# Mixing and turning heads in the middle of a weight block, and the last pooling passes cut off from GpSimd's adds and held in program order

## The chip, the core and the metric

The kernel runs on one core of one Trainium2 chip. The metric is device time in microseconds (us), the median of several runs. Five engines work side by side, each through its own list of instructions: TensorE (PE, matrix products), VectorE (DVE), ScalarE (ACT), GpSimd (POOL) and SyncE (SP, which issues the DMAs here).

## The reference, cut to what matters

One layer with 512 positions and 1024 channels. A normalised input `hn` is projected into three mixers (A, B, C) and three gates, the mixers' outputs are merged and projected, and a SwiGLU layer and a gated embedding follow. The change touches A and C.

```
# A: spatial gating, 8 heads of 128 channels, 4 blocks of 128 positions
u, v = split(gelu(z_sgu))
v = layer_norm(v, g_v, b_v)
mixed = einsum('hij,bnjhc->bnihc', w, v) + b_s      # one 128x128 matrix per head
br_a = (u * mixed) @ w_sgu_out
# B: depthwise convolution, width 31: 31 multiply-adds ("taps") per channel tile
# C: pooling with windows 2, 4, 8, 16 on four groups of 256 channels
outs.append((c - prev) / cnt - zf)                  # trailing mean minus the input
br_c = (einsum('bsgc,gcd->bsgd', pooled, w_pool) * s_pool) @ w_pool_out
...
merged = gates[0] * br_a + gates[1] * br_b + gates[2] * br_c
```

## The kernel before, in words

Channels lie on the 128 partitions, so a tile of a product is 128 channels by 512 positions. Every float32 operand of a product is split into a rounded part `hi` (a cast on ACT) and the rest `lo` (a subtraction on DVE), and each product is three matmuls (hi·hi, hi·lo, lo·hi: `mm3`). Weights stream in blocks of 128x1024: a DMA into `raw`, then `split` into `hi` and `lo`. A weight block is 24 matmuls.

The instructions are written by a scheduler: it takes the program in the order in which it is written, estimates times, and may reorder instructions on an engine, except where `order()` (or `drain`) keeps them in program order. On the chip, each engine then runs its list as it stands. Nearly all lines show as L69, that of the helper that issues them, so the names of tiles tell the steps apart.

- `natural` (L433) computes the two halves of A, `v_all` first and `u_all` second, with positions on the partitions. For each half of the columns (`c` = 0, 1) it holds four PSUM banks `ps_nat`, one per block of positions, and takes four weight blocks (`kk` = 0 to 3). After each weight block it drains some convolution taps from `background`, and yields.
- `v_all` is normalised on DVE (`v_norm`, `v_gain`), and GpSimd adds the bias (`v_all<-v_all,b_bc`), while the products of `u_all` run.
- `mix_head(h)` splits one head of `v_all` (`v_split`, hi on ACT, lo on DVE), multiplies it with the head's matrix (`ps_mix`, three matmuls) and lets DVE form `gated` from it. `turn_head(h)` transposes `gated` on PE (`ps_tr`, four small matmuls) and splits it (`sgu`). Heads 0 to 3 are mixed, and 0 and 1 turned, inside `natural` for `u_all` at `c` = 1, the rest between the gate tiles that follow (`ps_gate`).
- For C, `z_all` is computed in eight tiles (`ps_z`). After each pair, `pool_windows` (L570) lets GpSimd add shifted copies (`win`, 1 to 4 adds and as many small copies, for windows 2 to 16). Then three passes on DVE divide, and subtract `z_all`: two short ones for the first positions (`win<-win,rcnt` and `win<-win,z_all` of a few elements) and a long one (128x2x510 down to 128x2x496). `win` is then split into `pl_hi` and `pl_lo`, and `pool_map` multiplies that with the group's weights (`ps_pool`, twelve matmuls, of which the first two need `pl_hi` alone, and ten stand together behind them).
- The taps of the convolution (`acc<-h_conv,vec,acc`, DVE, one tile of 512 positions each) fill up DVE: 4 are drained after each block in `u_all`, 3 after a `z` tile, 5 after a gate tile. `drain` puts them in program order. When a tile is done, GpSimd adds it to `conv_sum`.

Of the kernel before, what the change touches and what calls it, by code (L numbers as in the profile page):

```python
# [13 lines left out]
ALU = mybir.AluOpType  # L14
# [7 lines left out]
NB = T // P  # L22
# [4 lines left out]
WINDOWS = (2, 4, 8, 16)  # L27
GROUPS = (0, 1, 2, 3)
# [53 lines left out]
def hybrid_block(  # L82
# [8 lines left out]
    order = InOrder(tc)  # L91
    dve, act_e, pe = order.engine(nc.vector), order.engine(nc.scalar), order.engine(nc.tensor)
# [9 lines left out]
    def bank(name):  # L102
        return psum.tile([P, T], F32, tag="ps", name=name)

    def wide_tile(name):
        return wide.tile([P, KT, T], F32, tag="wide", name=name)

    def slot(tag, name, dt=F32R, shape=(2, T)):
        return act.tile([P, *shape], dt, tag=tag, name=name, bufs=6 if tag == "tm" else 8)

    def t2(name, n=T):
        return tmp.tile([P, n], F32, tag="t2", name=name)
# [23 lines left out]
    def col(name, k):  # L136
        i = VECS.index(name) * KT + k
        return vec[:, i:i + 1]
# [23 lines left out]
    def split(hi, lo, src):  # L162
        act_e.copy(hi, src)
        dve.tensor_tensor(out=lo, in0=src, in1=hi, op=ALU.subtract)

    def split_scaled(hi, lo, src, scale):

        act_e.activation(out=hi, in_=src, func=AF.Copy, scale=scale)
        dve.scalar_tensor_tensor(out=lo, in0=src, scalar=scale, in1=hi,
                                       op0=ALU.mult, op1=ALU.subtract)  # L170
# [36 lines left out]
    def mm3(out, wh, wl, xh, xl, first, last):  # L207
        pe.matmul(out, lhsT=wh, rhs=xh, start=first, stop=False)
        pe.matmul(out, lhsT=wh, rhs=xl, start=False, stop=False)
        pe.matmul(out, lhsT=wl, rhs=xh, start=False, stop=last)  # L210
# [4 lines left out]
    def product(ps, w, acts, hs=FULL, k0=0, last=True):  # L215

        hi, lo = w
        for i, a in enumerate(acts):
            mm3(ps[:, hs], blk(hi, i), blk(lo, i), a[:, 0, hs], a[:, 1, hs],
                k0 + i == 0, last and i == len(acts) - 1)  # L220
# [11 lines left out]
    def drain(n):  # L232
        for _ in range(min(n, len(background))):
            with order():
                background.pop(0)()
# [72 lines left out]
    POOL_LAG = 3  # L308
# [107 lines left out]
    for i in range(KT):  # L416
        t = t2("nrm")
        dve.scalar_tensor_tensor(out=t, in0=x_all[:, i], scalar=col("g_mix_pre", i),
                                       in1=x_inv, op0=ALU.mult, op1=ALU.mult)
# [13 lines left out]
    def natural(dst, evacuate, taps):  # L433

        for c in range(2):
            banks = [bank("ps_nat") for _ in range(NB)]
            for kk in range(4):
                hi, lo = weights.get()
                for b in range(NB):
                    ts = slice(b * P, (b + 1) * P)  # L440
                    for j in range(2):
                        k = 2 * kk + j
                        a = hn[k]
                        ws = slice(j * T, (j + 1) * T)
                        pe.matmul(banks[b], lhsT=a[:, 0, ts], rhs=hi[:, ws],
                                         start=k == 0, stop=False)
                        pe.matmul(banks[b], lhsT=a[:, 1, ts], rhs=hi[:, ws],
                                         start=False, stop=False)
                        pe.matmul(banks[b], lhsT=a[:, 0, ts], rhs=lo[:, ws],
                                         start=False, stop=k == KT - 1)  # L450
                drain(taps)
                if kk == 3:
                    for b in range(NB):
                        evacuate(dst, b, c, banks[b])
                yield c, kk

    def blocks_of(t):
        return t.rearrange("p a b -> p (a b)").rearrange("p (n c) -> p n c", n=NB)
# [13 lines left out]
    for _ in natural(v_all, v_gelu, TAPS[1]):  # L472
        pass
# [31 lines left out]
    def mix_head(h):  # L505
        cs = slice(h * P, (h + 1) * P)
        vs = slot("tm", "v_split", shape=(2, NB, P))
        split(vs[:, 0], vs[:, 1], v_all[:, :, cs])
        ps = bank("ps_mix")
        mm3(ps, sg_hi[:, cs], sg_lo[:, cs], vs[:, 0], vs[:, 1], True, True)  # L510
        gated[h] = t2("gated")
        with order():
            dve.scalar_tensor_tensor(
                out=gated[h].rearrange("p (n c) -> p n c", n=NB),
                in0=ps.rearrange("p (n c) -> p n c", n=NB),
                scalar=col("b_sgu_s", h), in1=u_all[:, :, cs], op0=ALU.add, op1=ALU.mult)

    def turn_head(h):
        pt = bank("ps_tr")
        for b in range(NB):  # L520
            bs = slice(b * P, (b + 1) * P)
            pe.transpose(out=pt[:, bs], in_=gated[h][:, bs], identity=ident)
        sgu_T[h] = slot("br", f"sgu{h}")
        split(sgu_T[h][:, 0], sgu_T[h][:, 1], pt)

    for c, kk in natural(u_all, u_gelu, TAPS_U):
        if c == 1:
            if kk > 1:
                turn_head(kk - 2)
            mix_head(kk)  # L530


    merged = wide_tile("merged")
# [1 line left out]
    def gate_tile(dst, taps, between=None):  # L535
        ps = bank("ps_gate")
        w = weights.get()
        half = KT // 2 if between else KT
        product(ps, w, hn[:half], last=not between)
        if between:  # L540
            between()
            product(ps, [h[:, half * P:] for h in w], hn[half:], k0=half)
        act_e.activation(out=dst, in_=ps, func=AF.Sigmoid)
        drain(taps)
# [21 lines left out]
    z_all = wide_tile("z_all")  # L566
    pool_T = [None] * KT
    pooled = [None] * 4

    def pool_windows(gi):  # L570
        w = WINDOWS[gi]
        z = z_all[:, 2 * gi:2 * gi + 2, :]
        cur, d = z, 1
        while d < w:
            nxt = slot("tm", "win", F32)
            nc.gpsimd.tensor_tensor(out=nxt[:, :, d:], in0=cur[:, :, d:], in1=cur[:, :, :T - d], op=ALU.add)
            nc.gpsimd.tensor_copy(nxt[:, :, :d], cur[:, :, :d])
            cur, d = nxt, 2 * d
        head = rcnt[:, None, :w].broadcast_to([P, 2, w])
        dve.tensor_tensor(out=cur[:, :, :w], in0=cur[:, :, :w], in1=head, op=ALU.mult)  # L580
        dve.tensor_tensor(out=cur[:, :, :w], in0=cur[:, :, :w], in1=z[:, :, :w], op=ALU.subtract)
        dve.scalar_tensor_tensor(out=cur[:, :, w:], in0=cur[:, :, w:], scalar=1.0 / w,
                                       in1=z[:, :, w:], op0=ALU.mult, op1=ALU.subtract)
        hi = slot("tm", "pl_hi")
        lo = slot("tm", "pl_lo")
        split(hi, lo, cur)
        pooled[gi] = hi, lo

    def pool_map(gi):
        wh, wl = weights.get()  # L590
        hi, lo = pooled[gi]
        for j in range(2):
            n = 2 * gi + j
            ps = bank("ps_pool")
            for k in range(2):
                s = slice(k * 256 + j * P, k * 256 + (j + 1) * P)
                mm3(ps, wh[:, s], wl[:, s], hi[:, k], lo[:, k], k == 0, k == 1)
            pool_T[n] = slot("br", f"pool{n}")
            split_scaled(pool_T[n][:, 0], pool_T[n][:, 1], ps, col("s_pool", n))

    for g in GROUPS:
        for n in (2 * g, 2 * g + 1):
            ps = bank("ps_z")
            product(ps, weights.get(), hn)
            act_e.copy(z_all[:, n, :], ps)
            drain(TAPS[3])
        pool_windows(g)
        if 0 < g < GROUPS[-1]:
            pool_map(g - 1)

    gates = []
    for n in range(KT + POOL_LAG):
        if n < KT:
            gates.append(t2("gate"))
            gate_tile(gates[n], TAPS[4], (lambda: pool_map(GROUPS[-2])) if n == 0 else None)
        if n == POOL_LAG - 1:
            pool_map(GROUPS[-1])
        if n >= POOL_LAG:
            i = n - POOL_LAG
            ps = branch_tile(pool_T, TAPS[4])  # L620
            t = t2("br")
            dve.tensor_tensor(out=t, in0=ps, in1=gates[i], op=ALU.mult)
            nc.gpsimd.tensor_tensor(out=merged[:, i, :], in0=merged[:, i, :], in1=t, op=ALU.add)
# [94 lines left out]
    with order():  # L718
# [6 lines left out]
        for i in range(N_HALF):  # L725
            n = KT - N_HALF + i
            add_mixed(mix_tile(n, late[i], lo_half), n, lo_half)
        sqs = []
        for i in range(N_HALF):
            n = KT - N_HALF + i  # L730
# [71 lines left out]
    def evacuate(ps, n, hs):  # L802
        act_e.activation(out=o2_all[:, n, hs], in_=ps[:, hs], func=AF.Copy, scale=col("g_ffn_post", n))
        add_square(f_sums[:, hs], ps[:, hs], n, dve)
# [32 lines left out]
    with order():  # L837
# [3 lines left out]
        w = weights.get(1)  # L841
        for b, hs in zip(halves, HALVES):
            ffn_out(b, KT - 1, 0, w, hs)
        w = weights.get(1)
        ffn_out(ps, KT - 2, 1, w)
        weights.ahead(3)
        w = weights.get(2)
# [41 lines left out]
        for n in range(N_LAST, KT):  # L889
            w = weights.get()  # L890
# [70 lines left out]
```

## Time and profile before

| | |
|---|---|
| median of 3 runs | 984.22 us (984.08 to 984.52) |
| the profiled execution | 983.63 us, of which the span from the first instruction to the last is 981.9 us |
| granted TensorE clock | 1.000 over the span |
| PE busy | 973.8 us (99%), 4682 matmuls |
| DVE busy | 677.3 us (69%), 903 instructions |
| ACT busy | 346.1 us (35%) |
| POOL busy | 88.2 us (9%), 64 instructions |
| DMA | 100.53 MB, mean 102 GB/s |

In a line of the timeline the columns are the start, the duration, the engine, the line in the code, the operation with the tile written and the tiles read, shapes, the number of merged instructions, and in brackets the idle time of the engine ahead of it and what ended that. The list of waits gives total us, number of waits and the longest.

### The profile page before, as it was taken

The numbers are of one execution on the slowest core, as the hardware profiler recorded it, in microseconds if no ns is written. First come the engines' busy times: TensorE is split into PE (matmuls) and PEld (weight loads), VectorE is DVE, ScalarE is ACT, GpSimd is POOL, SyncE is SP. The second block draws the span as 40 slices with busy tenths as digits, with TensorE's granted clock in tenths as the row PEclk, the third lists the DMA queues.
The fourth block names the chain that finished last, engine by engine and source line by source line (L and its number), as shares of the span: only waits on it lengthen the run. The fifth ranks groups of instructions, "written<-read, shape, count | busy, mean of one in ns | idle before, by whom it ended". The sixth has DMA issues, their size and how long they took to land.

```text
span 981.9 us, 11718 instructions
## 1 busy us (share of the span) xinstructions
PE 973.8 (99%) x4682; PEld 819.2 (83%) x4682; DVE 677.3 (69%) x903; ACT 346.1 (35%) x483; POOL 88.2 (9%) x64
## 2 busy tenths in 40 slices
PE   9999999999999999999999999999999999999998
PEld 6788888788888878888888998888888888888897
DVE  7898789999988899957555787544444432223575
ACT  6422333332224332146435443323232322223442
POOL 4000004000013712160000010000000000000000
PEclk9999999999999999999999999999999999999999
DMA  6433331323322322332338112323322333334312
GB/s 233 137 108 107 109 106 65 107 69 104 107 81 81 101 103 86 105 110 68 126 96 272 62 38 74 104 90 104 98 96 93 98 91 104 92 92 139 109 43 86
DMA packets 30006, 100.53 MB, mean 102 GB/s; under 512 B 3456, under 2 KB 3968, under 8 KB 29952
## 3 DMA queue, kind: packets, MB, share of 16 engines
q1 hardware_dynamic: 29808, 99.75, 30.9%
q8 instruction: 36, 0.59, 0.2%
q14 instruction: 18, 0.15, 0.0%
q10 hardware_dynamic: 144, 0.04, 0.0%
HBM read 97.68 MB, written 2.10 MB: 102 GB/s over the span
## 4 chain that ended last, share of the span: by engine, by line
PE 88%; DVE 7%; issue 2%; DMA 1%; ACT 1%; SPq 0%; DVEq 0%; ACTq 0%
PE ps_f L69 25%; PE ps_br L69 13%; PE ps_fo L69 12%; PE ps_gate L69 12%; PE ps_ag L69 5%; PE ps_pg L69 5%; PE ps_o L69 5%; PE ps_z L69 4%; PE ps_nat L69 4%; DVE lo L69 2%; DVE acc L69 2%; PE ps_ple L69 1%; PE ps_pool L69 1%; DVE v_all L69 1%; DMA first_all<-in_w_first 1%
## 5 line engine op out<-in xcount | busy, mean ns | idle before, releaser
L69 ACT CAST hi<-raw 128x1024 fp32r<-128x1024 f32 (+3 forms) x158 | 162.5, 1030 | 456.3 <-PE ps_br L69 88.4
L69 DVE TENSOR_TENSOR lo<-raw,hi 128x1024 fp32r<-128x1024 f32 (+3 forms) x158 | 206.2, 1306 | 107.0 <-ACT hi L69 106.5
L69 DVE SCALAR_TENSOR_TENSOR acc<-h_conv,vec,acc 128x511 f32<-128x511 f32 (+14 forms) x240 | 183.3, 764 | 5.2
L69 PE MATMUL ps_f<-hg,hi 128*128 128x512 f32 (+1 forms) x624 | 184.5, 379 | 0.0
L69 PEld LDWEIGHTS ps_f<-hg,hi 128*128 128x128 f32 x624 | 115.1, 188 | 21.7
L69 PE MATMUL ps_gate<-hn,hi 128*128 128x512 f32 x384 | 119.6, 392 | 0.9 <-DVE gated L69 0.9
L69 PE MATMUL ps_f<-hg,lo 128*128 128x512 f32 (+1 forms) x312 | 118.0, 379 | 0.0
L69 PE MATMUL ps_fo<-f,hi 128*128 128x512 f32 (+1 forms) x396 | 111.0, 366 | 0.0
L69 PEld LDWEIGHTS ps_gate<-hn,hi 128*128 128x128 f32 x384 | 72.0, 188 | 17.1 <-DVE gated L69 1.3
L69 PEld LDWEIGHTS ps_fo<-f,hi 128*128 128x128 f32 x396 | 71.7, 189 | 12.2
L69 PE MATMUL ps_nat<-hi,hn 128*128 128x512 f32 x256 | 78.8, 390 | 0.0
L69 PE MATMUL ps_gate<-hn,lo 128*128 128x512 f32 x192 | 74.9, 390 | 0.0
L69 PE MATMUL ps_fo<-f,lo 128*128 128x512 f32 (+1 forms) x198 | 72.5, 366 | 0.0
L69 PEld LDWEIGHTS ps_f<-hg,lo 128*128 128x128 f32 x312 | 58.7, 188 | 11.0
L69 PEld LDWEIGHTS ps_nat<-hi,hn 128*128 128x128 f32 x256 | 48.1, 188 | 10.0
L69 DVE TENSOR_TENSOR f<-ps_f,h_inv 128x512 f32<-128x512 f32 x22 | 15.2, 690 | 56.5 <-PE ps_f L69 56.5
L69 PE MATMUL ps_nat<-lo,hn 128*128 128x512 f32 x128 | 49.9, 390 | 0.0
L69 PE MATMUL ps_ag<-hn,hi 128*128 128x512 f32 x160 | 49.6, 391 | 0.2 <-DVE sig L69 0.2
L69 PEld LDWEIGHTS ps_fo<-f,lo 128*128 128x128 f32 x198 | 37.4, 189 | 6.0
L69 PEld LDWEIGHTS ps_gate<-hn,lo 128*128 128x128 f32 x192 | 36.1, 188 | 7.5
L69 DVE TENSOR_TENSOR silu<-ps_f,h_inv 128x512 f32<-128x512 f32 x22 | 15.2, 690 | 36.0 <-PE ps_f L69 35.9
L69 PE MATMUL ps_br<-pool,hi 128*128 128x512 f32 x128 | 39.6, 389 | 0.0
(214 smaller groups left out, 1566.5 us busy)
## 6 DMA issues: line engine op xcount, KB each, us to landing
raw<-in_w_mix SPq DMA_DIRECT2D x90, 512.0 KB, 3.2
raw<-in_w_ffn_in SPq DMA_DIRECT2D x44, 512.0 KB, 3.3
raw<-in_w_ffn_out SPq DMA_DIRECT2D x16, 448.0 KB, 3.3
raw<-in_w_ffn_out SPq DMA_DIRECT2D x8, 512.0 KB, 3.5
raw<-in_w_ple_gate SPq DMA_DIRECT2D x8, 512.0 KB, 4.2
x_all<-in_xT SPq DMA_DIRECT2D x8, 256.0 KB, 6.4
h_all<-in_xT SPq DMA_DIRECT2D x4, 512.0 KB, 5.2
out_dram<-pg SPq DMA_DIRECT2D x7, 256.0 KB, 2.0
```

The costliest lines, as they stand in the source:

```text
L69: inst = op(*args, **kw)
```

## The change

`natural` yields in the middle of a weight block, ahead of the third of its four blocks of positions, where it yielded at the end of it. What the loop over `u_all` does at a yield comes twelve matmuls (half a block) earlier in the program. In that loop `mix_head` stands ahead of `turn_head`.

`pool_windows` keeps only GpSimd's adds. The three DVE passes and the split move to a new function, `pool_mean`, and are held in program order. They are called later: for group 0 after the z tile 2, for group 1 after tile 4, for group 2 after tile 7, and for group 3 after the gate tile 1, each time behind the taps that this tile drained.

```
             for kk in range(4):
                 hi, lo = weights.get()
                 for b in range(NB):
+                    if b == NB // 2:
+                        yield c, kk
                     ts = slice(b * P, (b + 1) * P)
...
-                yield c, kk
...
         if c == 1:
+            mix_head(kk)
             if kk > 1:
                 turn_head(kk - 2)
-            mix_head(kk)
...
             cur, d = nxt, 2 * d
+        pooled[gi] = cur
+
+    def pool_mean(gi):
+        w = WINDOWS[gi]
+        z, cur = z_all[:, 2 * gi:2 * gi + 2, :], pooled[gi]
         head = rcnt[:, None, :w].broadcast_to([P, 2, w])
-        dve.tensor_tensor(out=cur[:, :, :w], in0=cur[:, :, :w], in1=head, op=ALU.mult)
-        dve.tensor_tensor(out=cur[:, :, :w], in0=cur[:, :, :w], in1=z[:, :, :w], op=ALU.subtract)
-        dve.scalar_tensor_tensor(out=cur[:, :, w:], in0=cur[:, :, w:], scalar=1.0 / w,
-                                       in1=z[:, :, w:], op0=ALU.mult, op1=ALU.subtract)
+        with order():
+            dve.tensor_tensor(out=cur[:, :, :w], in0=cur[:, :, :w], in1=head, op=ALU.mult)
+            dve.tensor_tensor(out=cur[:, :, :w], in0=cur[:, :, :w], in1=z[:, :, :w], op=ALU.subtract)
+            dve.scalar_tensor_tensor(out=cur[:, :, w:], in0=cur[:, :, w:], scalar=1.0 / w,
+                                           in1=z[:, :, w:], op0=ALU.mult, op1=ALU.subtract)
         hi = slot("tm", "pl_hi")
         lo = slot("tm", "pl_lo")
         split(hi, lo, cur)
...
             drain(TAPS[3])
+            if g and n == 2 * g + (g == GROUPS[-1]):
+                pool_mean(g - 1)
         pool_windows(g)
...
             gate_tile(gates[n], TAPS[4], (lambda: pool_map(GROUPS[-2])) if n == 0 else None)
+        if n == POOL_LAG - 2:
+            pool_mean(GROUPS[-1])
         if n == POOL_LAG - 1:
             pool_map(GROUPS[-1])
```

No instruction is added or taken away, and the lists of SP (DMAs) and GpSimd keep their order. On PE, DVE and ACT rows move. In the rows below a name is the tile written, then the tiles read; a minus is a row of before, a plus one of the change.

PE, in the first weight block of `c` = 1 of `u_all`, the first mix (head 0):

```order
 L69 MATMUL ps_nat<-hi,hn_228 128x512 x2
 L69 MATMUL ps_nat<-lo,hn_228 128x512
-L69 MATMUL ps_nat<-hi,hn_227 128x512 x2
+L69 MATMUL ps_mix<-v_split,w_hi 128x512
+L69 MATMUL ps_nat<-hi,hn_227 128x512
+L69 MATMUL ps_mix<-v_split,w_hi 128x512
+L69 MATMUL ps_mix<-v_split,w_lo 128x512
+L69 MATMUL ps_nat<-hi,hn_227 128x512
 L69 MATMUL ps_nat<-lo,hn_227 128x512
 L69 MATMUL ps_nat<-hi,hn_228 128x512 x2
```

The three `ps_mix` matmuls stood behind all 24 matmuls of the block; now the first stands behind 12 of them, and the other two behind 13. On ACT and DVE the splits of the first two heads keep their places.

DVE, the passes of group 2 (window 8), before:

```order
L69 SCALAR_TENSOR_TENSOR pool_2449<-ps_pool,vec,pool_2449 128x512
L69 SCALAR_TENSOR_TENSOR acc_225<-h_conv_221,vec,acc_225 128x485
L69 TENSOR_TENSOR lo<-raw,hi 128x512
L69 SCALAR_TENSOR_TENSOR win<-win,z_all 128x2x504
L69 TENSOR_TENSOR win<-win,rcnt 128x2x8
L69 SCALAR_TENSOR_TENSOR acc_225<-h_conv_221,vec,acc_225 128x484
L69 TENSOR_TENSOR win<-win,z_all 128x2x8
L69 SCALAR_TENSOR_TENSOR acc_225<-h_conv_221,vec,acc_225 128x483
L69 SCALAR_TENSOR_TENSOR acc_225<-h_conv_221,vec,acc_225 128x482
L69 TENSOR_TENSOR pl_lo<-win,pl_hi 128x1024
```

and in the change (`pool_2432` and `pool_2442` are the two results of group 1's `pool_map`):

```order
L69 SCALAR_TENSOR_TENSOR pool_2432<-ps_pool,vec,pool_2432 128x512
L69 TENSOR_TENSOR lo<-raw,hi 128x1024
L69 SCALAR_TENSOR_TENSOR acc_225<-h_conv_221,vec,acc_225 128x486
L69 TENSOR_TENSOR lo<-raw,hi 128x512
L69 SCALAR_TENSOR_TENSOR pool_2442<-ps_pool,vec,pool_2442 128x512
L69 SCALAR_TENSOR_TENSOR acc_225<-h_conv_221,vec,acc_225 128x485
L69 SCALAR_TENSOR_TENSOR acc_225<-h_conv_221,vec,acc_225 128x484
L69 SCALAR_TENSOR_TENSOR acc_225<-h_conv_221,vec,acc_225 128x483
L69 SCALAR_TENSOR_TENSOR acc_225<-h_conv_221,vec,acc_225 128x482
L69 TENSOR_TENSOR win<-win,rcnt 128x2x8
L69 TENSOR_TENSOR lo<-raw,hi 128x1024
L69 TENSOR_TENSOR win<-win,z_all 128x2x8
```

The long pass (128x2x504) is the next row. It moved behind the tile's last three taps (`acc` 484 to 482), and the last of these lets GpSimd add to `conv_sum`.

DVE, the passes of group 3 (window 16), before:

```order
L69 SCALAR_TENSOR_TENSOR pool_2584<-ps_pool,vec,pool_2584 128x512
L69 TENSOR_SCALAR acc_226<-h_conv_222,vec 128x512
L69 SCALAR_TENSOR_TENSOR acc_226<-h_conv_222,vec,acc_226 128x511
L69 SCALAR_TENSOR_TENSOR acc_226<-h_conv_222,vec,acc_226 128x510
L69 SCALAR_TENSOR_TENSOR win<-win,z_all 128x2x496
L69 TENSOR_TENSOR win<-win,rcnt 128x2x16
L69 SCALAR_TENSOR_TENSOR acc_226<-h_conv_222,vec,acc_226 128x509
L69 TENSOR_TENSOR win<-win,z_all 128x2x16
```

and in the change, where ahead of these rows stand `pool_2567`, a `lo` of 128x512, `pool_2577` (group 2's results), the first tap 128x512, a `lo` of 128x1024 and the taps 511 to 509:

```order
L69 SCALAR_TENSOR_TENSOR acc_226<-h_conv_222,vec,acc_226 128x508
L69 SCALAR_TENSOR_TENSOR acc_226<-h_conv_222,vec,acc_226 128x507
L69 TENSOR_TENSOR lo<-raw,hi 128x1024
L69 SCALAR_TENSOR_TENSOR acc_226<-h_conv_222,vec,acc_226 128x506
L69 SCALAR_TENSOR_TENSOR acc_226<-h_conv_222,vec,acc_226 128x505
L69 SCALAR_TENSOR_TENSOR acc_226<-h_conv_222,vec,acc_226 128x504
L69 SCALAR_TENSOR_TENSOR acc_226<-h_conv_222,vec,acc_226 128x503
L69 TENSOR_TENSOR win<-win,rcnt 128x2x16
L69 SCALAR_TENSOR_TENSOR acc_226<-h_conv_222,vec,acc_226 128x502
L69 TENSOR_TENSOR win<-win,z_all 128x2x16
L69 SCALAR_TENSOR_TENSOR win<-win,z_all 128x2x496
```

The long pass stood behind three taps of this tile and stands behind eleven. On PE the first `ps_pool` of group 3 keeps its place, right behind the third gate tile. The ten matmuls of group 2's `ps_pool` moved up toward it: with them, 58 matmuls stood from their first to group 3's first, and 37 stand there now. From the ten of group 1 to the first of group 2 there are 59, and from the ten of group 0 to the first of group 1 there are 46 (the ten counted in).

## The prediction

> **What bounds the kernel now.** I read the page first, then the waits of TensorE (PE), then the timeline at the places of the change, engine by engine.
>
> ```profile
> span 981.9 us, 11718 instructions
> PE 973.8 (99%) x4682; PEld 819.2 (83%) x4682; DVE 677.3 (69%) x903; ACT 346.1 (35%) x483; POOL 88.2 (9%) x64
> PE 88%; DVE 7%; issue 2%; DMA 1%; ACT 1%; SPq 0%; DVEq 0%; ACTq 0%
> ```
>
> PE is busy for 99% of the span and makes 88% of the chain that ended last. So time can only come from PE's waits or go into new ones. Its own list of waits, and a row of the chain that gives the pace:
>
> ```profile
> PE ps_gate L69 <- DVE gated L69: 0.9, 1, 0.9
> PE ps_pool L69 <- ACT pl_hi L69: 0.8, 1, 0.8
> PE ps_mix L69 <- DVE v_split L69: 0.2, 1, 0.2
> 221.00 5.44 PE ps_br L69 x24
> ```
>
> 24 matmuls in 5.44 us is 0.227 us each; with that pace I count how late the next matmul starts, which is a little more than these rows say. The three waits are where the change works, and all that it could win. What it could lose is larger: each moved row on PE or DVE can meet an operand that is not there yet.
>
> **The first mix.** PE, then the three engines that feed it:
>
> ```profile
> 163.80 0.62 PE L69 MATMUL ps_nat<-hi,hn 128*128 128x512 f32 x2
> 166.52 0.39 PE L69 MATMUL ps_mix<-v_split,w_hi 128*128 128x512 f32 x1
> 167.06 0.50 PE L69 MATMUL ps_mix<-v_split,w_hi 128*128 128x512 f32 x1 [0.15 <-DVE v_split L69]
> 167.40 0.40 PE L69 MATMUL ps_mix<-v_split,w_lo 128*128 128x512 f32 x1
> 161.28 2.78 POOL L489 TENSOR_TENSOR v_all<-v_all,b_bc 128x1024 f32<-128x1024 f32 x1 [2.83 <-DVE v_all L69]
> 161.06 3.55 DVE L69 SCALAR_TENSOR_TENSOR acc<-h_conv,vec,acc 128x511 f32<-128x511 f32 x2
> 164.09 1.15 ACT L69 CAST v_split<-v_all 128x512 fp32r<-128x512 f32 x2 [6.29 <-POOL v_all L489]
> 164.53 1.22 DVE L69 TENSOR_TENSOR lo<-raw,hi 128x1024 fp32r<-128x1024 f32 x1
> 166.32 0.68 DVE L69 TENSOR_TENSOR v_split<-v_all,v_split 128x512 fp32r<-128x512 f32 x1
> ```
>
> Before, PE reaches the first `ps_mix` at 166.52 and loses 0.32 us at the second (0.54 instead of 0.23 after the first) and 0.11 us behind it (0.34), in all 0.43 us. Its operand, DVE's `v_split`, ends at 167.00. Nothing on that way moves: GpSimd's last bias add ends at 164.06, ACT casts then, and DVE has a weight's `lo` and a tap ahead of `v_split`, in the same order as before. PE's list moves by 12 matmuls: it gets to the first `ps_mix` at 166.52 - 12 x 0.227 = 163.80, before GpSimd is done. One product stands between the two; the second mix still can't start before 167.06. Before, 11 more products were done by then, so PE is 11 x 0.227 = 2.5 us behind. This costs +2.5 us net of the old wait. It could only be less if `v_split` came earlier, and no row ahead of it moved; I keep 2.3 to 2.7.
>
> **The gate tile behind the products.**
>
> ```profile
> 186.70 0.40 PE L69 MATMUL ps_mix<-v_split,w_lo 128*128 128x512 f32 x1
> 188.01 0.73 PE L69 MATMUL ps_gate<-hn,hi 128*128 128x512 f32 x2 [0.91 <-DVE gated L69]
> 187.21 0.74 DVE L69 SCALAR_TENSOR_TENSOR gated<-ps_mix,vec,u_all 128x512 f32<-128x512 f32 x1
> ```
>
> The gate tile's bank is freed by DVE reading an earlier mix, which is late: 1.31 us from start to start instead of 0.23, and 0.11 behind it, 1.2 us lost. In the change 12 products (2.7 us) stand between the last mix and turn and the gate tile, and the mixes stand ahead of the turns, so the bank's reader has more time than it lacked. I take -1.2 us; the other end is 0, if DVE falls behind by the same 1.2. The turned heads' splits on ACT move too: ACT is 35% busy, and their first reader (`ps_br`) comes more than 30 us later, so they cost nothing. The taps drained after each block stay where they were in the program. SP issues the same DMAs in the same order.
>
> **The pooling passes.** The start of the ten `ps_pool` of a group, what follows it, and the wait before group 3:
>
> ```profile
> 319.21 0.39 PE L69 MATMUL ps_pool<-pl_lo,hi 128*128 128x512 f32 x1
> 320.55 0.69 ACT L69 ACTIVATE pool<-ps_pool,vec 128x512 fp32r<-128x512 f32 x1 [2.96 <-PE ps_pool L69]
> 321.27 0.75 DVE L69 SCALAR_TENSOR_TENSOR pool<-ps_pool,vec,pool 128x512 fp32r<-128x512 f32 x1 [2.90 <-ACT pool L69]
> 348.45 0.39 PE L69 MATMUL ps_gate<-hn,lo 128*128 128x512 f32 x1
> 348.53 1.04 ACT L69 CAST pl_hi<-win 128x1024 fp32r<-128x1024 f32 x1 [3.78 <-DVE win L69]
> 349.63 0.73 PE L69 MATMUL ps_pool<-pl_hi,hi 128*128 128x512 f32 x2 [0.79 <-ACT pl_hi L69]
> ```
>
> DVE ends the first result of a group's products 322.02 - 319.21 = 2.81 us after the ten start. The old wait before group 3 is 1.18 - 0.23 = 0.95 and 0.11 behind it: 1.1 us. The bracket at 321.27 shows too that DVE stood idle for 2.90 us with taps behind that row which needed nothing from PE: its list is not passed over.
>
> In the change, DVE's list from group 2's first result to group 3's long pass is fixed, so that PE's own ten products start a clock. Durations of its rows:
>
> ```profile
> 327.25 0.68 DVE L69 TENSOR_TENSOR lo<-raw,hi 128x512 fp32r<-128x512 f32 x1
> 159.47 0.53 DVE L69 TENSOR_SCALAR acc<-h_conv,vec 128x512 f32<-128x512 f32 x1
> 344.94 1.54 DVE L69 SCALAR_TENSOR_TENSOR acc<-h_conv,vec,acc 128x511 f32<-128x511 f32 x2
> 346.39 1.19 DVE L69 SCALAR_TENSOR_TENSOR win<-win,z_all 128x992 f32<-128x992 f32 x1
> 347.49 0.19 DVE L69 TENSOR_TENSOR win<-win,rcnt 128x32 f32<-128x32 f32 x1
> ```
>
> `lo` 0.68, second result 0.74, first tap 0.53, `lo` 1.22, five taps at 0.77 (3.85), `lo` 1.22, four taps (3.08), short pass 0.19, tap 0.74, short pass 0.19, long pass 1.19: 13.6 us. A row that needs nothing of the one ahead starts some 0.08 us before that ends (the short pass at 347.49 starts 0.09 before the long one is through), nine times, -0.7. With 2.81 ahead, 0.15 for the first `lo`, whose cast waits for the tenth product, ACT's 1.04 and 0.15 for two hand-overs: 17.0 us from the first of the ten to group 3's first `ps_pool`. PE has 37 matmuls there, 8.4 us. It waits **8.6 us** where it waited 1.1: +7.5. GpSimd's adds for group 3 run from 333.52 to 344.95 before (rows below), 11.4 us, and end ahead of DVE's first pass; they no longer set the time. If they reach into DVE's chain, it becomes longer.
>
> Group 2's passes go the same way, from group 1's ten: 2.81, `lo` 1.22, tap 0.77, `lo` 0.68, result 0.74, four taps 3.1, short pass 0.19, `lo` 1.22, short 0.19, long 1.19, less 0.6, and ACT's 1.04 with 0.15: 12.7 us against 59 matmuls, 13.4. This would be covered by 0.7 us, but two of GpSimd's adds fall in between: the last tap releases `conv_sum`, and group 3's first add is queued behind it. What such adds do to DVE:
>
> ```profile
> 331.36 2.20 POOL L385 TENSOR_TENSOR conv_sum<-conv_sum,acc 128x512 f32<-128x512 f32 x1 [5.91 <-DVE acc L69]
> 332.33 2.32 DVE L69 TENSOR_TENSOR lo<-raw,hi 128x1024 fp32r<-128x1024 f32 x1
> 333.52 2.87 POOL L576 TENSOR_TENSOR win<-z_all 128x1022 f32<-128x1022 f32 x1
> 336.60 1.89 POOL L576 TENSOR_TENSOR win<-win 128x1020 f32<-128x1020 f32 x1
> 336.63 2.93 DVE L69 TENSOR_TENSOR lo<-raw,hi 128x1024 fp32r<-128x1024 f32 x1 [1.99 <-ACT hi L69]
> 344.55 0.40 POOL L577 COPY win<-win 128x16 f32<-128x16 f32 x1
> 322.58 2.81 DVE L69 TENSOR_TENSOR lo<-raw,hi 128x1024 fp32r<-128x1024 f32 x1 [0.56 <-ACT hi L69]
> ```
>
> A `lo` of 1.22 us takes 2.32 beside `conv_sum` and 2.93 beside a window add: DVE is held 1.1 and 1.7 us, and in the change its short and long pass come right there. 12.7 + 2.8 + 0.3 (an estimate, for a small copy that ends group 2's own adds) is 15.8: PE waits 2.4 us. The ends are 0 (both adds elsewhere) and 4.0 (one more hold of 1.6, as the `lo` at 322.58 had). For group 1 the list is 2.81, `lo` 0.68, tap, result 0.74, two taps, short pass, `lo` 1.22, tap, short and long pass, and the cast, 10.6 us against 46 matmuls, 10.4: I take 0.3, between 0 and a hold of 1.7. Group 0 has more than a tile of slack.
>
> **The sum.** +2.5 - 1.2 + 0.3 + 2.4 + 7.5 = +11.5 us on the profiled execution's 983.63, or 995.1; that execution lies 0.6 below the median of 984.22, so 995.7.
>
> One thing is left: PE stands idle for 8.6 us in one piece, and no wait of before is near that. What PE does after standing idle, only the start shows:
>
> ```profile
> 0.00:5.00 5.00, 3.59 (x8) 1.03 (x8) 0.80 (x4) 2.57 (x4) 0.79 (x7) 1.00 0.62 167
> 5.00:9.30 4.30, 3.81 (x9) 3.04 (x10) 3.38 (x6) 3.40 (x7) 0.00 (x0) 1.00 0.94 335
> 9.30:25.00 15.70, 15.70 (x70) 12.78 (x68) 15.47 (x13) 10.74 (x18) 9.18 (x6) 1.00 0.61 232
> ```
>
> The first eight matmuls take 3.59 us and the next nine fill 4.30, then 70 take 15.70: half the pace for the first 17. At 0.227 they would have taken 3.9, so a start from rest costs up to 4.0 us. Whether a pause in the middle does so too, no row shows: 0 to 4.0. I take 1.9, about the middle, since the pause is as long as that whole slow start but PE is fed densely behind it. Forecast: **997.6 us**.
>
> [...]
>
> **The rivals.**
> - *The clock holds.* The stalls come as counted and PE goes on at 0.227: 995.7. For it: PE's rows show one pace from 9.3 us on, through waits up to 1.2 us. Against it: none of these is near 8.6. [...]
> - *Faster: the waits go and none comes.* The old 0.43 + 1.2 + 1.1 fall away: 984.22 - 2.7 = 981.5. The place is group 3: DVE would have to reach the end of the long pass within 8.4 - 2.81 - 1.2 = 4.4 us of group 2's result. There are 13 us of rows in its list; against it speaks every one of them.
> - *The held passes cost nothing, the mix does.* If the taps ahead of the passes ran in DVE's idle time, +2.5 - 1.2 and no more: 985.5, within what can be told from no change (0.2%, 2.0 us). It decides at the same point as the one above.
> - *The small stalls are covered.* Groups 1 and 2 cost nothing and the clock holds: 984.22 + 2.5 - 1.2 + 7.5 = 993.0.
> - *It goes on.* Full price for the restart (4.0), group 2's 4.0 and group 1's 1.7: 984.22 + 2.5 - 1.2 + 1.7 + 4.0 + 7.5 + 4.0 = 1002.7.
>
> **How the numbers follow.** Forecast 0.55 (995.5 to 1001), clock holds 0.27 (about 994 to 997), small stalls covered 0.05, beyond 1001 0.07, faster 0.03, mix alone 0.03. The range 992.5 to 1001 leaves out the last three, 0.13. Slower by over 0.2%: 0.94; within 0.2%: 0.03; faster: 0.03.
>
> **What would show it.** Right: PE waits for `pl_hi` some 8 to 9 us before group 3 and 1 to 3 before group 2, for `v_split` twice, 2.8 us in all, and the wait for `gated` is gone; matmuls start 0.43 us apart for some us behind the longest wait. Wrong: the longest wait for `pl_hi` under 5 us, which would say that DVE came through its taps faster than its rows, or that a row that I take as fixed was passed over.

## The result and the profile after

| kernel | median, us | lowest to highest, runs | ratio to before |
|---|---|---|---|
| before | 984.52 | 984.08 to 984.94, 5 | |
| changed | **998.48** | 997.11 to 1000.2, 5 | 1.0142, 95% interval 1.0128 to 1.0155 |

The change makes the kernel 14.0 us (1.4%) slower. The forecast was 997.6, with a range of 992.5 to 1001, which holds every single run. The profiled run took 999.32 us. Its page first, the lines that answer to those of before, and the line of the granted clock in 40 slices of 24.9 us:

```profile
span 997.5 us, 11721 instructions
PE 977.9 (98%) x4682; PEld 820.8 (82%) x4682; DVE 673.8 (68%) x903; ACT 346.7 (35%) x483; POOL 85.0 (9%) x64
PEclk9999999999999979999999999999999999999999
PE 89%; DVE 6%; issue 2%; DMA 1%; ACT 1%; POOL 0%; SPq 0%; DVEq 0%; ACTq 0%
```

The span grew by 15.6 us. PE has the same 4682 matmuls and is yet 4.1 us longer busy: some of them ran slower, and the clock line has a 7 in the fifteenth slice. The other 11.5 us must be waits. (The three instructions more are none of those that the second line counts.) TensorE's list of waits for the operands that the change touches:

```profile
PE ps_pool L69 <- ACT pl_hi L69: 10.2, 2, 8.4
PE ps_mix L69 <- DVE v_split L69: 1.6, 1, 1.6
...
PE ps_mix L69 <- ACT v_split L69: 0.8, 1, 0.8
```

The wait for `gated` (0.9) has left the list. The wait for `pl_hi` grew from 0.8 to 10.2 in two pieces, and `v_split` is waited for twice.

**The first mix**, PE and then DVE. In brackets stands PE's idle time and what ended it:

```profile
163.80 0.39 PE L69 MATMUL ps_nat<-lo,hn 128*128 128x512 f32 x1
164.97 0.50 PE L69 MATMUL ps_mix<-v_split,w_hi 128*128 128x512 f32 x1 [0.78 <-ACT v_split L69]
165.31 0.40 PE L69 MATMUL ps_nat<-hi,hn 128*128 128x512 f32 x1
167.27 0.80 PE L69 MATMUL ps_mix<-v_split,w_hi 128*128 128x512 f32 x1 [1.56 <-DVE v_split L69]
167.86 0.63 PE L69 MATMUL ps_mix<-v_split,w_lo 128*128 128x512 f32 x1
166.54 0.68 DVE L69 TENSOR_TENSOR v_split<-v_all,v_split 128x512 fp32r<-128x512 f32 x1
```

DVE's `v_split` starts at 166.54, 0.22 later than before, which is the distance by which this whole run lags at that point. The second mix starts 0.05 us behind its end, as before; PE alone came earlier. New is what begins with the last PE row: matmuls follow one another by 0.43 us (167.86, 168.29, 168.71), where the pace is 0.227.

**Group 2**, PE, GpSimd and DVE:

```profile
338.17 0.39 PE L69 MATMUL ps_gate<-hn,lo 128*128 128x512 f32 x1
340.30 0.74 PE L69 MATMUL ps_pool<-pl_hi,hi 128*128 128x512 f32 x2 [1.74 <-ACT pl_hi L69]
333.84 1.29 POOL L385 TENSOR_TENSOR conv_sum<-conv_sum,acc 128x512 f32<-128x512 f32 x1 [6.08 <-DVE win L69]
335.09 2.87 POOL L577 TENSOR_TENSOR win<-z_all 128x1022 f32<-128x1022 f32 x1
334.02 2.19 DVE L69 TENSOR_TENSOR lo<-raw,hi 128x1024 fp32r<-128x1024 f32 x1 [0.17 <-ACT hi L69]
336.13 1.86 DVE L69 TENSOR_TENSOR win<-win,z_all 128x16 f32<-128x16 f32 x1
337.91 1.20 DVE L69 SCALAR_TENSOR_TENSOR win<-win,z_all 128x1008 f32<-128x1008 f32 x1
```

GpSimd's `conv_sum` and `win` run beside DVE's `lo` (2.19 instead of 1.22 us) and beside its short pass of 16 elements (1.86 instead of 0.19). The long pass starts at 337.91, just as GpSimd's add ends (335.09 + 2.87 = 337.96).

**Group 3**, PE from the first of group 2's ten products, then DVE and ACT:

```profile
345.68 0.39 PE L69 MATMUL ps_pool<-pl_lo,hi 128*128 128x512 f32 x1
...
353.84 0.39 PE L69 MATMUL ps_gate<-hn,lo 128*128 128x512 f32 x1
362.65 1.22 PE L69 MATMUL ps_pool<-pl_hi,hi 128*128 128x512 f32 x2 [8.42 <-ACT pl_hi L69]
356.41 3.08 DVE L69 SCALAR_TENSOR_TENSOR acc<-h_conv,vec,acc 128x506 f32<-128x506 f32 x4
...
360.28 1.18 DVE L69 SCALAR_TENSOR_TENSOR win<-win,z_all 128x992 f32<-128x992 f32 x1
361.56 1.05 ACT L69 CAST pl_hi<-win 128x1024 fp32r<-128x1024 f32 x1 [5.97 <-DVE win L69]
```

PE starts the gate tile's last matmul at 353.84 and the next one only at 362.65. DVE is busy until the long pass ends at 361.46, in the main with taps of the convolution that stand ahead of that pass; then ACT casts.

**The clock.** Stretches of the changed kernel: start and end, length, busy time of PE, PEld, DVE, ACT and POOL (in brackets instructions), the granted clock, DMA:

```profile
163.59:167.00 3.41, 1.33 (x5) 0.47 (x3) 3.41 (x4) 2.70 (x6) 0.68 (x1) 1.00 0.08 8
167.00:170.42 3.41, 3.15 (x7) 2.51 (x8) 3.41 (x7) 2.40 (x4) 0.00 (x0) 0.50 0.42 148
170.42:173.83 3.41, 3.41 (x16) 2.82 (x15) 3.41 (x5) 1.05 (x1) 0.00 (x0) 1.00 0.20 47
337.67:341.08 3.41, 1.68 (x7) 1.06 (x7) 2.25 (x3) 1.89 (x2) 3.33 (x4) 1.00 0.32 124
341.08:344.50 3.41, 3.41 (x16) 2.80 (x15) 2.25 (x2) 0.60 (x2) 3.33 (x3) 1.00 0.04 12
354.74:358.15 3.41, 0.00 (x0) 0.00 (x0) 3.34 (x5) 0.85 (x2) 0.00 (x0) 1.00 0.19 55
358.15:361.56 3.41, 0.00 (x0) 0.00 (x0) 3.38 (x7) 0.01 (x1) 0.00 (x0) 0.50 0.26 98
361.56:364.98 3.41, 2.32 (x6) 1.86 (x7) 3.34 (x5) 1.04 (x1) 0.00 (x0) 0.50 0.00 0
364.98:368.39 3.41, 3.41 (x10) 2.67 (x9) 0.47 (x1) 0.00 (x0) 0.00 (x0) 0.50 0.00 0
368.39:371.81 3.41, 3.41 (x16) 2.82 (x15) 0.00 (x0) 0.01 (x1) 0.00 (x0) 1.00 0.00 0
```

The clock is halved for 3.41 us at the first mix and for 10.24 us at group 3; 7 and 10 matmuls ran in a stretch that at full pace holds 15 or 16. Group 2's wait of 1.74 us (the two rows from 337.67) did not halve it.

### The profile page after: what moved, and what is told of

The parts are those of the page before. It is cut to its first block, busy times and chain, and to the rows that moved or that the text cites. A ratio compares the mean times of both kernels' runs of the same rounds, so it can differ in the third digit from the quotient of the medians.

```text
span 997.5 us, 11721 instructions
## 1 busy us (share of the span) xinstructions
PE 977.9 (98%) x4682; PEld 820.8 (82%) x4682; DVE 673.8 (68%) x903; ACT 346.7 (35%) x483; POOL 85.0 (9%) x64
## 4 chain that ended last, share of the span: by engine, by line
PE 89%; DVE 6%; issue 2%; DMA 1%; ACT 1%; POOL 0%; SPq 0%; DVEq 0%; ACTq 0%
PE ps_f L69 24%; PE ps_br L69 13%; PE ps_gate L69 12%; PE ps_fo L69 12%; PE ps_nat L69 6%; PE ps_ag L69 5%; PE ps_pg L69 5%; PE ps_o L69 4%; PE ps_z L69 4%; DVE lo L69 2%; PE ps_pool L69 1%; DVE acc L69 1%; PE ps_ple L69 1%; DVE v_all L69 1%; DMA first_all<-in_w_first 1%
## 5 line engine op out<-in xcount | busy, mean ns | idle before, releaser
L69 DVE TENSOR_TENSOR lo<-raw,hi 128x1024 fp32r<-128x1024 f32 (+3 forms) x158 | 202.0, 1279 | 107.2 <-ACT hi L69 105.8
L69 PEld LDWEIGHTS ps_nat<-hi,hn 128*128 128x128 f32 x256 | 48.5, 190 | 10.2
```

The lines of the kernel that those rows point to most:

```text
L69: inst = op(*args, **kw)
```

## The experiments

The theory: DVE's list, in the order in which it is written, sets the waits before the pooling products, at full length; the mix costs what its operand's own time costs; the rest of the loss is half pace of PE behind its waits. The rivals: that something else makes the waits (GpSimd's adds, the weights), that they overlap, or that the half pace is no cost of the waits. The experiments ran on two further chips, where the kernel before took 984.74 us (the first four; 10 runs, 983.8 to 988.1) and 985.23 us (the last four; 17 runs, 983.98 to 987.31).

### 1. The mix alone

```
 natural():     + if b == NB // 2: yield c, kk        - yield c, kk (at the end of the block)
 loop:          + mix_head(kk) ahead of turn_head      (pooling as before)
```

> The mix part of the change alone: the yield in the middle of the block and mix ahead of turn; the pooling as before. Theory (a moved row costs what its operand is late): PE waits 2.8 us at the first mix in place of 0.4, the wait for gated (1.2) is gone, and PE may go at half pace for up to 3.4 us behind the wait, as in the change (1.4 us lost): +1.3 to +2.7, 985.8 to 987.2. Rival (the mix costs nothing, all of the loss is in the pooling): -1.2, 983.3.

Measured: 987.92 us (987.21 to 988.59, 7 runs), ratio 1.0026 (1.0013 to 1.0039): 3.2 us slower by the medians, 2.6 by the ratio. The median lies a little above the range that was expected; by the ratio (984.52 x 1.0026 = 987.1) it lies inside. Both waits for `v_split` stand there as in the full change (0.8 and 1.6), the wait for `gated` is gone, the old wait before group 3 (0.8) is there. The clock is halved at the mix here too:

```profile
165.23:168.64 3.41, 1.07 (x4) 0.54 (x4) 3.41 (x5) 3.21 (x7) 0.18 (x1) 1.00 0.11 20
168.64:172.06 3.41, 3.41 (x9) 2.65 (x9) 3.41 (x7) 1.89 (x3) 0.00 (x0) 0.50 0.34 136
```

What follows: this part of the change is a loss by itself, +2.5 - 1.2 in waits and some 1.5 in half pace. (If the three passes are called late but not held in order, the scheduler puts them back, and each engine's list is row for row that of this experiment. So what the pooling part does comes from the hold. That version was not run by itself.)

### 2. The pooling passes alone

```
 pool_mean() with order(), and its later calls, as in the change
 natural():  yield at the end of the block;   loop: turn_head ahead of mix_head, as before
```

> The pooling part alone: passes called later and held in order; the yield as before. Theory: the waits before groups 1 to 3 come as in the change (0.3, 2.1, 8.6 in place of 1.1) whether the mix has moved or not, and the half pace behind the longest one: +12 to +13, 996.5 to 997.5. Rival (PE's lateness from the mix made the pooling waits longer): clearly less, under 994.

Measured: 997.32 us (995.82 to 998.76, 4 runs), ratio 1.0126 (1.0109 to 1.0143), inside the range that the theory gave; the rival (under 994) falls. The wait for `pl_hi` is 10.2 us in two pieces, the longest 8.4, as in the full change, and the wait for `gated` (0.9) is back. The two parts alone add up to 15.8 us by the medians and 15.0 by the ratios, against 14.0 together; with intervals of +-1.3 and +-1.7 us this is no difference that can be told.

The same 8.4 us of waiting, and a shorter half pace than in the full change:

```profile
353.15:356.56 3.41, 0.00 (x0) 0.00 (x0) 3.34 (x5) 0.30 (x1) 0.00 (x0) 1.00 0.33 92
356.56:359.97 3.41, 0.00 (x0) 0.00 (x0) 3.38 (x7) 0.56 (x1) 0.00 (x0) 0.50 0.15 61
359.97:363.39 3.41, 2.87 (x7) 2.29 (x8) 3.27 (x5) 0.49 (x1) 0.00 (x0) 0.50 0.00 0
363.39:366.80 3.41, 3.41 (x17) 2.81 (x16) 0.00 (x0) 0.00 (x0) 0.00 (x0) 1.00 0.00 0
```

6.83 us here, 10.24 there.

### 3. PE kept busy ahead of group 3, and ahead of the mix too

```
 changed kernel, ahead of group 3's pool_map:
+    psf = psum.tile([P, T], F32, ...)
+    with order():
+        for _ in range(36):        # products of zeros, bf16, read by nobody
+            pe.matmul(psf, lhsT=warm_up[:, :P], rhs=warm_up, start=True, stop=True)
 second kernel: the same, and 11 such products ahead of the first mix_head
```

> The change with 36 matmuls of zeros, bf16, into a bank of their own, ahead of group 3's first ps_pool (8.2 us at full pace, to lie in the wait of 8.6). Theory (idling halves the pace): group 3's products start at the same time, but at full pace, 2.9 us faster than the change: about 995.6. Rival (the slow pace has another cause, such as what DVE does there): no gain, 998.5, with matmuls 0.43 us apart behind the wait.

> As the one before, and 11 such matmuls ahead of the first mix (2.5 us) too. Theory: neither wait leads to half pace, -2.9 and -1.4: about 994.2, granted clock 1.000, and the runs within 1 us of each other, where those of the change spread over 3.1. Rival (the wait at the mix, 1.7 us in its longest piece, is too short to matter): as the one before.

Measured: 996.63 us (996.29 to 997.89, 4 runs), ratio 1.0121 (1.0106 to 1.0136), with the products ahead of group 3; 996.04 us (995.58 to 997.14, 4 runs), ratio 1.0115 (1.01 to 1.013), with both. PE ahead of group 3 in the first of them:

```profile
353.73 7.94 PE L70 MATMUL ps_fill<-warm_up 128*128 128x512 bf16 x36
362.31 0.72 PE L70 MATMUL ps_pool<-pl_hi,hi 128*128 128x512 f32 x2 [0.64 <-ACT pl_hi L70]
362.87 0.63 PE L70 MATMUL ps_gate<-hn,hi 128*128 128x512 f32 x2
```

PE computes nothing of use for 7.94 us, `ps_pool` starts 8.8 us behind the start of the gate tile's last matmul (353.50 here), as in the changed kernel (353.84 to 362.65), and then goes on at full pace (from 362.87 its matmuls start 0.23 us apart; the mean granted clock of the run is 0.999, where the changed kernel's is 0.993). So the lost pace comes from PE's standing still. The two kernels came out 1.0 and 1.8 us above their expectations. These had been counted down from the changed kernel's 998.5, less 2.9 and 1.4 for the clock, about what its profiled run lost; but the median run loses less. Counted up from before, 984.74 + 11.3 of waits (table below) is 996.04, which is what was measured for the second; that it agrees to the last digit is chance. Its runs spread over 1.6 us at granted clocks of 0.998 to 1.000, where under 1 us and 1.000 had been expected, and it gains 0.6 us on the first, which intervals of +-1.5 us don't tell from nothing: that filling the mix's wait pays is not shown here. The first kernel's mix came through at full pace in the profiled run, though it waited as long as that of experiment 1:

```profile
163.78:167.19 3.41, 2.27 (x9) 1.24 (x7) 3.41 (x3) 1.76 (x4) 1.62 (x1) 1.00 0.00 0
167.19:170.61 3.41, 2.21 (x10) 1.83 (x11) 3.41 (x6) 3.34 (x6) 0.00 (x0) 1.00 0.46 156
```

### 4. Group 3's passes one gate tile earlier

```
-        if n == POOL_LAG - 2:
+        if n == POOL_LAG - 3:
             pool_mean(GROUPS[-1])
```

> The changed kernel, with group 3's three passes called one gate tile earlier, behind gate tile 0's taps: the long pass then stands about five rows, some 5 us, earlier in VectorE's list, and the rest is as it was. If VectorE's list ahead of the long pass sets the wait (my theory), the wait before group 3 falls from 8.6 to about 3.6 us and the half pace behind it shrinks to 0 to 1.7 us lost: 990 to 993 us, with the mix's wait and group 2's 2 us as before. If the wait comes from elsewhere (GpSimd's window adds or the weights), it stays near 8.6 us and the time near 998.

Measured: 993.73 us (992.83 to 995.63, 4 runs), ratio 1.0085 (1.0071 to 1.0099); on 985.23 of before, a little above the range that was expected, by its ratio (984.52 x 1.0085 = 992.9) inside. The waits for `pl_hi`:

```profile
PE ps_pool L69 <- ACT pl_hi L69: 5.3, 2, 3.5
```

The longest fell from 8.4 to 3.5 us. In DVE's list six rows fewer stand ahead of the long pass, five taps and a `lo`. In the changed kernel's list five taps and a `lo` ahead of that pass take 4.93 us (351.48 to 356.41), and the wait shrank by 4.9. So the wait is DVE's list, and each row ahead of the pass is paid in full. The half pace behind it was 3.41 us in the profiled run:

```profile
357.51:360.92 3.41, 0.90 (x4) 0.76 (x5) 3.41 (x6) 1.39 (x2) 0.00 (x0) 1.00 0.00 0
360.92:364.33 3.41, 3.41 (x10) 2.64 (x9) 3.31 (x5) 0.00 (x0) 0.00 (x0) 0.50 0.45 154
```

### 5. Without one of GpSimd's adds

```
-        elif k > 1:
+        elif k > 1 and k != 5:
             nc.gpsimd... conv_sum += acc        # tile 5's share is left out
```

> The changed kernel without GpSimd's one add of tile 5 to conv_sum (its share of the sum is left out of the output). If the two adds of GpSimd that fall on VectorE's lo and long pass make group 2's wait (my theory), the wait before group 2 falls from 1.9 us by the 1.0 to 1.3 us that the first of them holds VectorE, or goes wholly, since the next window add then comes earlier and meets other rows. If VectorE's rows alone set it, it stays at 1.9 us. Group 3's wait stays at 8.6 us either way; time 996 to 998.

One run, 999.04 us, above the 996 to 998 that were expected; a single run shows no difference in time, and ahead of group 2's product it is already 1.88 us behind the changed kernel's profiled run (the gate tile's last matmul starts at 340.05, there at 338.17). Its rows, GpSimd, DVE and PE:

```profile
336.43 2.44 POOL L577 TENSOR_TENSOR win<-z_all 128x1022 f32<-128x1022 f32 x1 [6.77 <-ACT z_all L69]
335.89 1.22 DVE L69 TENSOR_TENSOR lo<-raw,hi 128x1024 fp32r<-128x1024 f32 x1 [0.16 <-ACT hi L69]
337.04 1.86 DVE L69 TENSOR_TENSOR win<-win,z_all 128x16 f32<-128x16 f32 x1
341.21 0.72 PE L69 MATMUL ps_pool<-pl_hi,hi 128*128 128x512 f32 x2 [0.77 <-ACT pl_hi L69]
```

`lo` takes 1.22 us instead of 2.19, and PE's wait falls from 1.74 to 0.77: the same 0.97. The short pass is still held by the window add (1.86), which waits for `z_all` and so falls there anyway. So the first hold counts in full. The 0.77 that is left is less than the second hold (1.67), which this run keeps; that it would go with that hold is counted from the rows and was not run.

### 6. The mix behind 18 products instead of 12

```
 experiment 1 with
-                    if b == NB // 2:
+                    if b == 3:
```

> The mid-block mix alone (no held passes), with the yield ahead of the fourth of the four blocks of positions instead of the third: the first mix stands behind 18 of 24 products instead of 12. Theory: each product that stands ahead of it saves 0.227 us, so its wait of 2.7 us falls by 1.36, too short to halve the clock, which gives back the 1.45 us of half pace as well; the gate tile's wait stays gone: 984.5 to 985.5, level with before. Rival: the half pace does not hang on the length of the wait, and only 1.4 us come back: 986.3 to 986.8.

Measured: 985.1 us (984.08 to 986.58, 10 runs), ratio 1.0 (0.9991 to 1.0009), as the theory had it.

```profile
166.84 0.39 PE L69 MATMUL ps_mix<-v_split,w_hi 128*128 128x512 f32 x1
168.75 0.50 PE L69 MATMUL ps_mix<-v_split,w_hi 128*128 128x512 f32 x1 [1.51 <-DVE v_split L69]
```

and the stretch in which this wait lies:

```profile
166.70:170.12 3.41, 1.90 (x9) 1.26 (x8) 3.41 (x6) 3.41 (x7) 0.00 (x0) 1.00 0.43 154
```

The wait for the ACT half is gone, the one for the DVE half is there, and in the profiled run the clock holds. Against experiment 1 the later place gives back 3.3 us by the medians (+3.2 on its own chip, -0.1 here) and 2.6 by the ratios, with intervals of +-1.3 and +-0.9. Counted, it is 2.6: about 1.5 of half pace, and 1.1 of waiting, since the second mix, the one that waits for DVE, stands behind 18 products instead of 13. (The expectation had put the waiting at 1.36, for six products.)

### 7. Both old waits taken away

```
 kernel before, with
+YIELDS = ((), (0, 2), (2,), (3,))         # blocks of positions ahead of which natural yields, by weight block
+                    if b in YIELDS[kk]: yield c, kk
-                yield c, kk               # and mix_head ahead of turn_head, heads counted 0 to 3
-        if n == POOL_LAG - 1: pool_map(GROUPS[-1])     # behind the third gate tile
+        gate_tile(..., {..., POOL_LAG: lambda: pool_map(GROUPS[-1])}.get(n))   # amid the fourth
 (and the weights of group 3's product are asked for one gate tile later)
```

> The kernel before, with the first mix left at the end of its weight block, the later ones moved earlier inside theirs, the order of mixing and turning swapped, and group 3's product moved from behind the third gate tile into the middle of the fourth. Theory: the wait for gated goes (-1.2 us), the old wait for pl_hi goes (-1.06), no new one comes: 982 to 982.6 against 984.5. Rival: the moved mixes meet the bias adds of GpSimd or the turns wait for gated, and it stays at 984 or above.

Measured: 982.96 us (982.43 to 983.98, 7 runs), ratio 0.9975 (0.9963 to 0.9986): 2.3 us faster than before, which is what the two waits cost (1.2 and 1.1), and so it is faster than the kernel before and the changed one. Of the places of the change, one short wait is left:

```profile
PE ps_mix L70 <- DVE v_split L70: 0.2, 1, 0.2
```

Here the first mix stays where it was, since its operand is not ready earlier, and the later ones move; and the product goes to where its operand is, rather than the operand's making being held back.

## Why the prediction was right

The changed kernel's profiled run against that of before, by how much later the same matmul starts. (The last matmul of the third gate tile, for one: 348.45 before and 353.84 now, 5.39 later.)

| step | predicted, us | measured, us |
|---|---|---|
| first mix | +2.5 | +2.5 |
| gate tile's wait for `gated` | -1.2 | -1.2 |
| group 1 | +0.3 | +0.3 |
| group 2 | +2.4 | +2.1 |
| group 3 | +7.5 | +7.6 |
| **waits together** | **+11.5** | **+11.3** |
| half pace | +1.9 | 1.45 at the mix, 2.7 at group 3 |
| start of the run | 0 | +0.2 |

- *The mix.* Counted from the rows of the operand's makers, none of which moved, and right to 0.1. From start to start the two waits exceed the pace of 0.227 by 0.94 and 1.73, with 0.11 behind each (behind the second, half pace hides it here; in experiment 6 that is 168.75 to 169.08, less the pace); less the 0.43 of before, this is 2.46.
- *The gate tile.* The bound of 0 did not come in; experiment 1 shows the gain without the pooling passes.
- *Group 3.* From the first of group 2's ten products to group 3's first, 17.0 us were forecast, and 345.68 to 362.65 is 16.97. Experiment 4 shows that the rows of DVE's list are the cause, and that GpSimd's adds, which end at 347.80, before DVE's first pass at 359.40, are not.
- *Group 2.* Two holds of DVE, 1.1 and 1.7, were forecast on the short and the long pass; they were 0.97 and 1.67, on a `lo` and on the short pass. Their sum was about right (2.8 and 2.64), the rows were not, and that is luck in part. Experiment 5 shows the first of them.
- *The clock.* This term is mis-sized. It was put at 1.9, once, behind the longest wait, and came to 4.15 in the profiled run, above even the 4.0 that was its upper end: no half pace was counted behind the mix, where it cost 1.45, and behind group 3's wait it lasted 10.24 us, where the start's 7.9 us of it (the 3.59 and 4.30 us of its first 17 matmuls) was the measure, and cost 2.7. Over the runs it is 998.48 - 984.52 - 11.3 = 2.7. That the forecast came within 0.9 us of the median is luck in this term: 1.9 was taken as about the middle of 0 to 4.0, and no row of before could tell its size. Its size changes from run to run: the runs at a mean granted clock of 0.997, 0.995, 0.995, 0.993 and 0.993 took 997.11, 998.25, 998.48, 999.32 and 1000.2 us. The runs spread, in the main, as this term does.

The rival "the clock holds" (995.7) falls by these rows; experiment 3 shows that it would have given just about its own time, had PE been kept busy: 996.04. "Faster" and "the mix alone" fall by group 3's wait. "The small stalls are covered" falls by group 2's 2.1 us. "It goes on" falls by groups 1 and 2, which cost 0.3 and 2.1 us and not 1.7 and 4.0; its 4.0 for the restart was near the 4.15 that the profiled run lost to the clock.

## What to carry to other kernels

In these runs DVE, with its one list in a fixed order, paid every row that stood ahead of the one that was waited for (six rows, 4.9 us, in experiment 4): before holding a step "behind" other work, add up the rows from the last hand-over to it, and set them against the work that the waiting engine has in that stretch. Moving a consumer earlier pays only by as much as its operand is early (the first mix, twelve matmuls earlier, cost 2.5 us); where PE waits for an operand, try first to move the product to later, as in experiment 7. And count a wait of the matrix engine twice: for its own length, and for the half pace that may follow, even where no single wait is long: in the profiled run it cost 1.45 us behind the mix's two waits (0.78 and 1.56) and 2.7 behind the one of 8.42.

## What the runs showed of the hardware that was not expected

How long PE's clock stayed halved did not go by the length of the wait ahead of it. In the changed kernel it was halved for 3.41 us behind the mix's two waits (0.78 and 1.56) and for 10.24 behind group 3's 8.42; in experiment 2 for 6.83 behind a wait of 8.4, and in experiment 4 for 3.41 behind one of 3.5. These are one, three, two and one times 3.41 us, and the 187.73 us at full clock between the two falls of the changed kernel (170.42 to 358.15) are 55 times 3.413.

The 3.41 us just ahead of a fall held 1.33 and 0.00 us of PE's rows in the changed kernel, 1.07 in experiment 1, 0.00 in experiment 2 and 0.90 in experiment 4. Behind stretches of the same length with 1.68 us (337.67 in the changed kernel), 1.90 (experiment 6), 2.27 and 2.21 (experiment 3) the clock stayed full; and so it did behind this one of experiment 7, whose mean clock of 0.999 over 981.9 us leaves less than 3 us at half pace in the whole run:

```profile
38.56:41.98 3.41, 1.55 (x7) 0.94 (x5) 3.41 (x7) 3.12 (x6) 0.00 (x0) 1.00 0.05 18
```

Whether this amount of work is what decides, and how much of it, was not tested, and the ends of PE's rows are modelled. In experiment 2 the full clock came back behind 3.41 us at half pace with 7 matmuls (2.87 us); in the changed kernel the half pace went on behind 3.41 us with 6 (2.32).

The mix's waits of 0.8 and 1.6 us were followed by half the clock in the profiled runs of the changed kernel and of experiment 1, and by the full clock in that of experiment 3. What decides between the two was not shown. The kernel before has runs at a granted clock below 1.000 as well: on the chip of the first four experiments five runs at 1.000 took 983.8 to 984.78 us, and five at 0.996 to 0.998 took 984.67 to 988.1. None of the latter was profiled, so where their clock fell was not shown.
